# Last MLP layer of a hybrid decoder: down projections of seven blocks as seven quadrant products with tokens on partitions

## The chip, the cores and the metric

One core of a Trainium2 chip (trn2). The metric is the device time of one execution in microseconds, the median of the runs. All arithmetic is in float32: each operand of a large product is split into a high part (type fp32r) and the remainder, and a product is the sum of three matmuls (high x high, high x low, low x high).

## What is computed

Two layers on a residual stream `x` of 512 tokens x 1024 features: multi-head latent attention with its MLP, then gated linear attention with its MLP, then a final RMS norm. The change concerns the second MLP, the end of the mixer before it, and the final norm.

```python
def rms_norm(x, gain):
    y = x * rsqrt(mean(x * x, axis=-1) + EPS)
    return y * gain

def sq_relu_mlp(xn, w_up, w_down):          # w_up (1024, 4096), w_down (4096, 1024)
    hid = square(relu(xn @ w_up))
    return hid @ w_down

for i in range(2):
    x = x + mixer[i](rms_norm(x, norm_mix[i]))     # i = 1: ... @ gla_w_o
    x = x + sq_relu_mlp(rms_norm(x, norm_mlp[i]), mlp_w_up[i], mlp_w_down[i])
return rms_norm(x, final_norm)
```

## The kernel before

The residual stream lies in SBUF with features on partitions: eight tiles `xT[0..7]` of 128 features x 512 tokens, all in one tensor `xall`. The kernel is written in a tile framework: the text states operations and buffers, and a scheduler orders the instructions of each engine ahead of time by their place in the text and by a model of when their inputs are there. Each engine then works through its list in order. `bufs=n` on a tag means n buffers in turn; a new tile waits until the oldest one has been read for the last time.

Weights come with `load` (SyncE's queue, 1 MB, two buffers `wraw`). `piece` splits a part of them into `wh` and `wl` (three buffers each): ScalarE writes the high part (line 104), VectorE the low part (line 107). `mm3` is the three matmuls (lines 112 to 114).

An MLP goes through its 4096 hidden features in eight blocks of 512 (`FB`). For the first block, `up` is a plain product: four tiles of 128 hidden features, 8 x 3 matmuls of 512 tokens each. For the others, `up_fast` multiplies by quadrants: the block's weights (1024 features x 512 hidden) and the normed stream (1024 x 512 tokens) are both cut in four, and seven products of sums and differences of quadrants take the place of eight (Strassen's scheme in Winograd's form). The combinations of the stream, T1 to T4, are made once (`quadrants`), those of the weights by VectorE for each block (s1, s2, s4 and one in place). In one product, each high weight tile is multiplied by the high and low stream parts side by side (512 columns, line 923), each low weight tile by the high part alone (256 columns, line 924). The two halves of the result are added by ScalarE and VectorE on the way out of PSUM (`total`, lines 938 to 941); `finish` applies relu, the norm's factor and the square, and splits the hidden quadrant into its parts.

`down` of a block is a plain product: eight output tiles, each 4 x 3 matmuls of 512 tokens, and each is added to `xT` by VectorE (line 837). It is a generator: `up_fast` of block b+1 calls for its tiles at set places (`others`), so that TensorE always has one of the two to do. In the last block of the last MLP (`down_final`) the first 256 tokens stay with features on partitions and go through the final norm there; the other 256 are turned by transposes into PSUM and get the down products added with tokens on partitions (line 871). Class `Final` does both norms and stores two outputs that the host joins.

At the end of linear attention, `out_start` begins the output projection with two tiles for the first four feature tiles of its input, while the last two heads are still being normed and turned (`head_norm`, `gather`). `out_proj` does the rest of the eight tiles and adds them to `xT`.

Of the kernel before, what the change touches and what calls it, by code (L numbers as in the profile page):

```python
# [50 lines left out]
def trunk_kernel(ctx: ExitStack, tc: tile.TileContext, t_in: dict, out: bass.AP, out_row: bass.AP):  # L51
# [12 lines left out]
    BANKS = {False: {"a": 2, "b": 3, "c": 3}, True: {"b": 3, "c": 1}}  # L64
# [157 lines left out]
    class Norm:  # L222
# [38 lines left out]
        def finish(self):  # L261
            m = bank("c")
# [100 lines left out]
    def a_pair(psums, w, nrm):  # L363
        for k in range(ND):
            if k == 5:
                nrm.finish()
            for j in range(2):
                mm3(psums[j], cut(w[j], slice(None), k), nrm.out[k], k == 0, k == ND - 1)
# [394 lines left out]
    def out_start(w2d, X, n):  # L763
        raw = col_chunk(w2d, 0, 256)
        w = [piece(raw[:, :, j * P : (j + 1) * P], ND, P) for j in range(2)]
        ps_ = [bank("a"), bank("a")]

        def mms(ks):
            for k in ks:
                for j in range(2):  # L770
                    mm3(ps_[j], cut(w[j], slice(None), k), X[k], k == 0, k == ND - 1)

        mms(range(n))
        return ps_, lambda: mms(range(n, ND))

    def out_proj(w2d, X, nxt, begun=None):
        for c in range(4):
            if c == 0:
                ps_, rest = begun or out_start(w2d, X, 0)
                rest()  # L780
            else:
                raw = col_chunk(w2d, c * 256, 256)
                w = [piece(raw[:, :, j * P : (j + 1) * P], ND, P) for j in range(2)]
                ps_ = [bank("ac"[c % 2]), bank("ac"[c % 2])]
                for j in range(2):
                    a_type(ps_[j], w[j], X)
            for j in range(2):
                m = 2 * c + j
                DVE.tensor_tensor(xT[m], ps_[j], xT[m], ALU.add)
                nxt.add(m, xT[m])  # L790


    def mlp(layer, nrm, tag, nxt, final=False):
# [47 lines left out]

        def down_final(b, hid):
            W = []
            for c in range(2):
                raw = load(
                    w_dn[b * FB : (b + 1) * FB, c * 512 : (c + 1) * 512].rearrange("(k p) n -> p k n", p=P), 4, 512
                )
                for k in range(4):  # L850
                    w = both_parts()
                    split(raw[:, k], w[:, 0], w[:, 1])
                    W.append((w[:, 0], w[:, 1]))
            for m in range(ND):
                p = bank("b")[:, :TH]
                for k in range(4):
                    w = cut(W[m // 4 * 4 + k], slice(None), slice(m % 4 * P, (m % 4 + 1) * P))
                    mm3(p, w, cut(hid[k], slice(None), slice(0, TH)), k == 0, k == 3)
                DVE.tensor_tensor(xT[m][:, :TH], p, xT[m][:, :TH], ALU.add)
                nxt.add(m)  # L860
            for t in (2, 3):
                tk = slice(t * P, (t + 1) * P)
                ps_ = [bank("ac"[t % 2]) for _ in range(2)]
                for c in range(2):

                    for j in range(4):
                        PE.matmul(ps_[c][:, j * P : (j + 1) * P], xT[c * 4 + j][:, tk], ident, start=j == 0, stop=False, is_transpose=True, skip_group_check=True)
                    for k in range(4):
                        w, x = cut(hid[k], slice(None), tk), W[c * 4 + k]
                        for n, (a, b_) in enumerate(((w[0], x[0]), (w[0], x[1]), (w[1], x[0]))):  # L870
                            PE.matmul(ps_[c], a, b_, start=False, stop=k == 3 and n == 2, skip_group_check=True)  # L871
                    if (t, c) == (2, 0):
                        nxt.mean()
                    nxt.row(t, c, ps_[c])
                    if (t, c) == (2, 0):
                        nxt.finish()


# [110 lines left out]
        for b in range(NB):  # L989
# [10 lines left out]
            if final:  # L1000
                psum_layout(False)
                down_final(b, hid)
            else:
                for _ in down(b, hid):
                    pass


    def gla(layer, nrm, vtag, ytag):
# [377 lines left out]
        def heads():  # L1386
            for h in (0, 2):
# [33 lines left out]
                if h:  # L1421
                    begun.append(out_start(w_o, Y, 4))
# [82 lines left out]
    class Final:  # L1505
        def __init__(self):
            self.es = ExitStack()
            self.out = None

        def add(self, m):  # L1510
            if self.out is None:
                pool = self.pool = self.es.enter_context(tc.tile_pool(name="fin", bufs=1, reuse_waits="tile"))
                self.out = [pool.tile([P, 2, TH], F32, tag=f"o{c}", name=f"o{c}") for c in range(ND // 2)]
                self.gain = pool.tile([P, D], F32, name="fin_gain")
                SP.dma_start(self.gain, t_in["fin_row"].to_broadcast([P, D]))
                DVE.tensor_scalar(self.gain, self.gain, -0.5, None, ALU.mult)
            src = xT[m][:, :TH]
            if m == 0:
                self.acc = sb.tile([P, TH], F32, tag="acc", bufs=2, name=uname("acc"))
                ACT.activation(self.acc, src, AF.Square)  # L1520
            else:
                sq = tmp((P, TH))
                ACT.activation(sq, src, AF.Square)
                DVE.tensor_tensor(self.acc, self.acc, sq, ALU.add)
                if m == ND - 1:
                    self.sums = parts_of(self.acc, lambda: tmp((P, TH), F32R))
            ACT.activation(self.out[m // 2][:, m % 2], src, AF.Copy, scale=gcol("fin", m))

        def mean(self):
            self.ms = bank("b")[:, :TH]  # L1530
            for i in range(2):
                PE.matmul(self.ms, inv_dr, self.sums[i], start=i == 0, stop=i == 1)

        def finish(self):
            r = sb.tile([P, TH], F32, tag="rstd", bufs=2, name=uname("rstd"))
            rsqrt(r, self.ms, TH)
            o_out = out.rearrange("(j p) t -> p j t", p=P)
            for c in range(ND // 2):
                y = self.out[c]
                for j in range(2):  # L1540
                    DVE.tensor_tensor(y[:, j], y[:, j], r, ALU.mult)
# [85 lines left out]
```

## Time and profile before

| | |
|---|---|
| median of three runs | 1083.77 us (1083.42 to 1083.77) |
| profiled execution | 1084.2 us, its span 1082.2 us |
| granted TensorE clock, mean | 0.998 |
| TensorE busy | 1072.8 us (99%) |
| VectorE busy | 864.5 us (80%) |
| ScalarE busy | 556.2 us (51%) |
| GpSimd busy | 43.7 us (4%), all in the first fifth |
| read from HBM | 98.35 MB, 93 GB/s over the span |

The span runs from the first to the last instruction; the profiled execution's own time is 2.0 us longer. PE is TensorE's matmuls, PEld its weight loads, DVE VectorE, ACT ScalarE, POOL GpSimd, SP SyncE. A row of instructions has the line of the kernel, the engine, the operation, output<-inputs with their shapes, the count, and then busy microseconds and mean nanoseconds of one. Matmuls overlap, so that their single durations add up to more than the time that passes.

### The profile page before, as it was taken

How to read it: one execution, taken by the hardware profiler on the slowest of the kernel's cores; microseconds unless marked ns; L12 is line 12 of the kernel's file. 1: busy time of each engine (PE TensorE's matmuls, PEld its weight loads, DVE VectorE, ACT ScalarE, POOL GpSimd, SP SyncE). 2: the span in 40 equal slices, each digit the busy share in tenths (PEclk: the TensorE clock that was granted, in tenths of full speed). 3: DMA queues.
4: the chain of work that ended last, by engine and by line, in shares of the span. 5: the costliest groups of instructions: out<-in, count | busy, mean ns of one | idle time of the engine just before them, and what ended most of it. 6: DMA issues, size and time to landing. Idle time of an engine off the chain costs nothing.

```text
span 1082.2 us, 14050 instructions
## 1 busy us (share of the span) xinstructions
PE 1072.8 (99%) x5352; PEld 906.4 (84%) x5352; DVE 864.5 (80%) x1446; ACT 556.2 (51%) x947; POOL 43.7 (4%) x72
## 2 busy tenths in 40 slices
PE   9999999999999999999999999999999999999997
PEld 8888888888888888888888888888888888888886
DVE  7899968987887877977686497569888797797885
ACT  7767654553453454445345565655445345344354
POOL 8310002000000000000000000000000000000000
PEclk9999999999999999999999999999999999999999
DMA  7311232142332332322222222142233233223222
GB/s 225 88 50 39 79 115 81 49 146 78 117 117 78 116 118 78 91 86 97 88 78 78 78 78 78 41 154 76 80 117 117 78 109 121 82 80 127 67 98 78
DMA packets 86195, 101.61 MB, mean 94 GB/s; under 512 B 7440, under 2 KB 64016, under 8 KB 86128
## 3 DMA queue, kind: packets, MB, share of 16 engines
q1 hardware_dynamic: 84320, 99.67, 28.3%
q10 hardware_dynamic: 1808, 1.05, 0.3%
q8 instruction: 42, 0.69, 0.3%
q14 instruction: 25, 0.20, 0.1%
HBM read 98.35 MB, written 2.10 MB: 93 GB/s over the span
## 4 chain that ended last, share of the span: by engine, by line
PE 96%; DVE 2%; ACT 1%; DMA 0%; issue 0%; SPq 0%; DVEq 0%; ACTq 0%
PE ps L114 20%; PE ps L112 20%; PE ps L113 20%; PE ps L923 17%; PE ps L924 9%; PE ps L1199 2%; PE ps L129 1%; PE ps L408 1%; PE ps L871 1%; PE ps L1326 1%; PE ps L1249 0%; PE ps L671 0%; PE ps L667 0%; PE ps L670 0%; PE ps L669 0%; DMA gains<-in_gains_dram 0%
## 5 line engine op out<-in xcount | busy, mean ns | idle before, releaser
L112 PE MATMUL ps<-set,wh 128*128 128x512 f32 x760 | 296.6, 390 | 1.1 <-DVE g L1349 0.8
L113 PE MATMUL ps<-set,wh 128*128 128x512 f32 x760 | 296.5, 390 | 0.0
L114 PE MATMUL ps<-set,wl 128*128 128x512 f32 x760 | 296.1, 390 | 0.0
L104 ACT ACTIVATE wh<-wraw 128x1024 fp32r<-128x1024 f32 x139 | 147.0, 1061 | 226.8 <-PE ps L113 114.4
L107 DVE TENSOR_TENSOR wl<-wraw,wh 128x1024 fp32r<-128x1024 f32 x139 | 169.5, 1220 | 34.7 <-ACT wh L104 34.6
L112 PEld LDWEIGHTS ps<-set,wh 128*128 128x128 f32 x760 | 142.6, 188 | 31.2 <-DVE g L1349 1.1
L114 PEld LDWEIGHTS ps<-set,wl 128*128 128x128 f32 x760 | 142.7, 188 | 30.2
L113 PEld LDWEIGHTS ps<-set,wh 128*128 128x128 f32 x760 | 142.8, 188 | 27.6
L923 PE MATMUL ps<-T,wh 128*128 128x512 f32 x448 | 157.5, 391 | 0.0
L924 PE MATMUL ps<-T,wl 128*128 128x256 f32 x448 | 126.2, 282 | 0.0
L923 PE MATMUL ps<-set,wh 128*128 128x512 f32 x336 | 119.9, 397 | 0.0
L923 PEld LDWEIGHTS ps<-T,wh 128*128 128x128 f32 x448 | 84.1, 188 | 18.2
L924 PE MATMUL ps<-set,wl 128*128 128x256 f32 x336 | 94.2, 280 | 0.0
L107 DVE TENSOR_TENSOR wl<-comb,wh 128x1024 fp32r<-128x1024 f32 x42 | 51.3, 1222 | 47.2 <-ACT wh L104 47.2
L837 DVE TENSOR_TENSOR xT<-ps,xT 128x512 f32<-128x512 f32 x120 | 82.2, 685 | 6.7 <-PE ps L114 6.7
L104 ACT ACTIVATE wh<-comb 128x1024 fp32r<-128x1024 f32 x42 | 44.6, 1061 | 83.3 <-PE ps L923 81.8
L924 PEld LDWEIGHTS ps<-T,wl 128*128 128x128 f32 x448 | 84.6, 189 | 0.5
L923 PEld LDWEIGHTS ps<-set,wh 128*128 128x128 f32 x336 | 63.1, 188 | 15.1
L941 DVE TENSOR_TENSOR tmp<-ps,tmp 128x512 f32<-128x512 f32 x98 | 67.1, 685 | 0.9
L924 PEld LDWEIGHTS ps<-set,wl 128*128 128x128 f32 x336 | 63.4, 189 | 1.6
L104 ACT ACTIVATE wh<-raw 128x1024 fp32r<-128x1024 f32 x28 | 29.5, 1054 | 56.7 <-PE ps L923 55.8
L112 PE MATMUL ps<-wh,set 128*128 128x512 f32 x144 | 58.5, 407 | 0.0
(372 smaller groups left out, 1658.3 us busy)
## 6 DMA issues: line engine op xcount, KB each, us to landing
wraw<-in_mlp_w_up_dram SPq DMA_DIRECT2D x32, 1024.0 KB, 5.4
wraw<-in_mlp_w_down_dram SPq DMA_DIRECT2D x18, 1024.0 KB, 5.1
raw<-in_mlp_w_down_dram SPq DMA_DIRECT2D x14, 1024.0 KB, 5.0
wraw<-in_gla_w_in_dram SPq DMA_DIRECT2D x12, 1024.0 KB, 5.2
wraw<-in_mla_w_o_dram SPq DMA_DIRECT2D x4, 1024.0 KB, 5.2
wraw<-in_gla_w_o_dram SPq DMA_DIRECT2D x4, 1024.0 KB, 5.2
xT<-in_x_dram SPq DMA_DIRECT2D x6, 256.0 KB, 5.5
wraw<-in_mla_w_in_dram SPq DMA_DIRECT2D x3, 512.0 KB, 6.4
```

The lines of the kernel that those rows point to most:

```text
L104: order(ACT.activation(hi, src, AF.Copy))
L107: lo_eng.tensor_tensor(lo, src, f(hi), ALU.subtract)
L112: PE.matmul(psum, wh, xh, start=start, stop=False)
L113: PE.matmul(psum, wh, xl, start=False, stop=False)
L114: PE.matmul(psum, wl, xh, start=False, stop=stop)
L129: PE.transpose(psum, src, ident[: src.shape[0], : src.shape[0]])
L408: PE.matmul(p, w[:, i, j * P : (j + 1) * P], x, start=start, stop=stop)
L837: DVE.tensor_tensor(xT[m], p, xT[m], ALU.add)
L923: PE.matmul(o.rearrange("p (h t) -> p h t", h=2), wh, x, start=start and k == 0, stop=False, skip_group_check=True)
L924: PE.matmul(o[:, :TH], wl, x[:, 0], start=False, stop=k == KH - 1, skip_group_check=True)
L941: DVE.tensor_tensor(by_tile(r), high, by_tile(r), ALU.add)
L1199: PE.matmul(p[:, t - t0], k[:, t * P : (t + 1) * P], moving[:, t], start=True, stop=True)
```

## The change

The last MLP gets a function of its own, `mlp_last`; the first one keeps `mlp`.

- The hidden block is no longer split for a plain product. It stays as four quadrants (hidden half x token half, `Q`, two sets in turn), and the down projection of the first seven blocks is also done as seven products of quadrants, with the tokens as the stationary operand and 512 output features as the moving one. Its output therefore has tokens on partitions.
- The partial results of the seven blocks stay in SBUF in five running sums of 128 x 1024 (`S11`, `S12`, `SU`, `S21`, `S5`); four of them lie in the place of `xall`. The stream itself is first written to memory (`x_kept`) and read back in the seventh block.
- `step` does one block: the down products of block b and the up products of block b+1, fourteen in all, which alternate; the diff shows the first seven. The sums of Winograd's scheme that several outputs share are carried on inside PSUM: ScalarE copies a bank into another one (`y`, `w2`, `e`, `d`), and the next products go on adding there. `onto` does the same with a running sum from SBUF.
- In an up product, the high weight tile meets the high and the low part of the stream in two matmuls of 256 columns, and all three terms add up in one place of PSUM.
- Part of the weights' combinations is made while loading: a plain load by SyncE and then a load by GpSimd that adds (`accum_op`) into the same tile. Each tile is loaded again for the next block as soon as it has been read for the last time (`after`).
- The last block's down product is done with tokens on partitions for all tokens; the old stream is turned into PSUM, added to the sums and carried on from there. The final norm follows by rows, and there is one output.
- The out projection of linear attention begins with three tiles, in banks "b", "c" and "a"; the second load of weights is therefore kept for its second tile.

```diff
-    BANKS = {False: {"a": 2, "b": 3, "c": 3}, True: {"b": 3, "c": 1}}
+    BANKS = {False: {"a": 2, "b": 3, "c": 3}, True: {"b": 3, "c": 1}, "quad": {"u": 4}}
...
-    def out_start(w2d, X, n):
-        raw = col_chunk(w2d, 0, 256)
-        w = [piece(raw[:, :, j * P : (j + 1) * P], ND, P) for j in range(2)]
-        ps_ = [bank("a"), bank("a")]
+    def out_start(w2d, X, n, tags="aa"):
+        raws, w, ps_ = [], [], []
+        for m, tag in enumerate(tags):
+            if m % 2 == 0:
+                raws.append(col_chunk(w2d, m * P, 256))
+            w.append(piece(raws[-1][:, :, m % 2 * P : (m % 2 + 1) * P], ND, P))
+            ps_.append(bank(tag))
...
-                    begun.append(out_start(w_o, Y, 4))
+                    begun.append(out_start(w_o, Y, 4, "bca"))
...
+    def mlp_last(layer, nrm):
...
+        x_kept = dram.tile([P, ND, S], F32, name="x_kept")
+        SP.dma_start(x_kept, xall)
+
+        Q = [[[f(slot("B")) for _ in range(2)] for _ in range(2)] for _ in range(2)]
...
+        def comb():
+            return fast.tile([P, 2 * S], F32, tag="comb", bufs=6, name=uname("comb"))
...
+        def signed(src, hi, lo, sign):
+            ACT.activation(hi, src, AF.Copy, scale=sign)
+            DVE.scalar_tensor_tensor(lo, src, sign, f(hi), ALU.mult, ALU.subtract)
...
+        def finish(src, half, th, q):
+            r = tmp()
+            r_t = nrm.rstd[:, (first, second)[th]].unsqueeze(1).to_broadcast([P, 2, TH])
+            DVE.scalar_tensor_tensor(by_tile(r), by_tile(src), 0.0, r_t, ALU.min if half else ALU.max, ALU.mult)
+            ACT.activation(q[half][th], r, AF.Square)
...
+        def fetch(b, name):
+            if name in ("A1", "A2"):
+                c = int(name[1]) - 1
+                W[name] = col_chunk(w_up, (b + 1) * FB + c * 256, 256)
+                if c:
+                    POOL.dma_start(W[name][:, :KH], up_quadrant(b, 0, 0), accum_op=ALU.add)
+                return
+            q = up_quadrant if name == "S1" else down_quadrant
+            W[name] = t = by_k(comb(), KH if name == "S1" else 2)
+            plain, more = {
+                "d11": ((0, 0), None), "d12": ((0, 1), None), "d22": ((1, 1), None),
+                "S1": ((1, 1), (1, 0)), "dS1": ((1, 1), (1, 0)), "dS3": ((1, 0), (0, 0)),
+            }[name]
+            SP.dma_start(t, q(b, *plain))
+            if more:
+                POOL.dma_start(t, q(b, *more), accum_op=ALU.add)
+
+        def up_product(t, a, q, start):
+            w = piece(a, KH, 256)
+            for j in range(2):
+                o = t[:, j * TH : (j + 1) * TH]
+                for k in range(KH):
+                    wh, wl = cut(w, slice(None), k, slice(j * P, (j + 1) * P))
+                    xh, xl = quad[q][k][:, 0], quad[q][k][:, 1]
+                    for n, (a_, x_) in enumerate(((wh, xh), (wh, xl), (wl, xh))):
+                        PE.matmul(o, a_, x_, start=start and j == 0 and k == 0 and n == 0, stop=k == KH - 1 and n == 2, skip_group_check=True)
+
+        def down_product(t, a, parts, start):
+            wh, wl = piece(a, 2, 512)
+            for tt in range(2):
+                o = t[:, tt * 512 : (tt + 1) * 512]
+                for k in range(2):
+                    xh, xl = cut(parts, slice(None), slice(k * TH + tt * P, k * TH + (tt + 1) * P))
+                    for n, (x_, w_) in enumerate(((xh, wh[:, k]), (xh, wl[:, k]), (xl, wh[:, k]))):
+                        PE.matmul(o, x_, w_, start=start and k == 0 and n == 0, stop=k == 1 and n == 2, skip_group_check=True)
+
+        def step(b, q, r, after):
+            opening = b == 0
...
+            def begun(src, total):
+                if opening:
+                    ACT.activation(total, src, AF.Copy)
+                    return two_banks("e")
+                t = two_banks("e")
+                ACT.activation(t, src, AF.Copy)
+                return t
+            def add(total, t):
+                DVE.tensor_tensor(total, t, total, ALU.add)
+            def onto(tag, total, a, parts):
+                t = two_banks(tag)
+                if not opening:
+                    ACT.activation(t, total, AF.Copy)
+                down_product(t, a, parts, opening)
+                ACT.activation(total, t, AF.Copy)
...
+            z = bank("u")
+            up_product(z, a11, "11", True)
+            y = bank("u")
+            ACT.activation(y, z, AF.Copy)
+            d = two_banks("d")
+            down_product(d, d11, parts_of_quad(q11), True)
+            e = begun(d, S11)
+            up_product(y, a12, "21", False)
+            finish(y, 0, 0, r)
+            DVE.tensor_tensor(a11, s1, a11, ALU.add)
+            down_product(e, d12, parts_of_quad(q21), opening)
+            add(S11, e)
+            DVE.tensor_tensor(d11, ds1, d11, ALU.add)
+            DVE.tensor_tensor(q12, q22, q12, ALU.subtract)
+            DVE.tensor_tensor(q11, q11, q12, ALU.add)
+            up_product(z, a11, "T2", False)
+            u = tmp()
+            ACT.activation(u, z, AF.Copy)
+            DVE.tensor_tensor(a12, a11, a12, ALU.add)
+            down_product(d, d11, parts_of_quad(q11, -1.0), False)
+            e = begun(d, S12)
+            DVE.tensor_tensor(d12, d11, d12, ALU.add)
+            after("d11")
+            w = bank("u")
+            up_product(w, s1, "T1", True)
...
+        for b in range(NB - 1):
+            step(b, Q[b % 2], Q[(b + 1) % 2], ...)
...
+        def residual(t, c):
+            src = (S11, S12, S21, SU)[2 * c + t // 2][:, t % 2 * 512 : (t % 2 + 1) * 512]
+            p = bank("u")
+            for j in range(4):
+                m = 4 * c + j
+                tr(p[:, j * P : (j + 1) * P], kept[m // 2][:, m % 2, t * P : (t + 1) * P])
+            DVE.tensor_tensor(src, p, src, ALU.subtract if c else ALU.add)
...
+            ACT.activation(o, src, AF.Copy)
...
+        order = [(t, c) for c in range(2) for t in range(NT)]
+        residual(*order[0])
+        residual(*order[1])
+        for i, tc_ in enumerate(order):
+            if i + 2 < len(order):
+                residual(*order[i + 2])
+            row(*tc_)
...
-    fin = Final()
-    psum_layout(True)
-    mlp(1, n_mlp1, "B", fin, True)
-    fin.es.close()
+    psum_layout("quad")
+    mlp_last(1, n_mlp1)
```

More of the change, by code (lines that the diff above doesn't have):

```diff
@@ L793, in mlp, with add @@
-    def mlp(layer, nrm, tag, nxt, final=False):
+        ps_, raws, rest = begun or out_start(w2d, X, 0)
+        rest()
+        def add(m, p):
+            DVE.tensor_tensor(xT[m], p, xT[m], ALU.add)
+            nxt.add(m, xT[m])
+        for m, p in enumerate(ps_):
+            add(m, p)
+        for c in range(len(ps_) // 2, ND // 2):
+            raw = raws[c] if c < len(raws) else col_chunk(w2d, c * 256, 256)
+            tiles = range(max(2 * c, len(ps_)), 2 * c + 2)
+            done = [(piece(raw[:, :, m % 2 * P : (m % 2 + 1) * P], ND, P), bank("ac"[c % 2])) for m in tiles]
+            for w, p in done:
+                a_type(p, w, X)
+            for m, (w, p) in zip(tiles, done):
+                add(m, p)
```

314 lines of the change are left out of this document (189 added, 125 removed).

## The prediction

> **What bounds the kernel now.** I read the page's head and its chain of waits first, then the busy time by stretches of the last MLP layer, then the order of time on TensorE there.
>
> ```profile
> span 1082.2 us, 14050 instructions
> PE 1072.8 (99%) x5352; PEld 906.4 (84%) x5352; DVE 864.5 (80%) x1446; ACT 556.2 (51%) x947; POOL 43.7 (4%) x72
> PE 96%; DVE 2%; ACT 1%; DMA 0%; issue 0%; SPq 0%; DVEq 0%; ACTq 0%
> ...
> 890.00:931.00 41.00, 41.00 (x208) 34.87 (x207) 33.43 (x45) 18.19 (x27) 0.00 (x0) 1.00 0.30 103
> 1050.88:1075.83 24.95, 24.93 (x164) 22.42 (x162) 14.61 (x37) 10.71 (x28) 0.00 (x0) 1.00 0.17 62
> 1075.83:1082.20 6.37, 0.00 (x0) 0.00 (x0) 1.76 (x5) 1.70 (x5) 0.00 (x0) 0.70 0.23 89
> ```
>
> The stretch rows give length, then busy time of PE, PEld, DVE, ACT and POOL, then granted clock, DMA share and GB/s. In the MLP blocks TensorE has no idle time at full clock (41.00 of 41.00), and the chain that ended last is 96% matmuls. So a matmul removed is time saved, as long as VectorE (33.4 of 41) and ScalarE (18.2) still deliver in time.
>
> A busy matmul overlaps the next one, so I price matmuls by the distance between starts.
>
> ```profile
> 683.58 0.39 PE L112 MATMUL ps<-wh,set 128*128 128x512 f32 x1
> 688.80 0.40 PE L114 MATMUL ps<-wh,set 128*128 128x512 f32 x1
> ...
> 761.21 0.39 PE L923 MATMUL ps<-set,wh 128*128 128x512 f32 x1
> ...
> 1040.21 0.39 PE L112 MATMUL ps<-set,wh 128*128 128x512 f32 x1
> 1050.42 0.39 PE L112 MATMUL ps<-set,wh 128*128 128x512 f32 x1
> 1051.10 0.28 PE L112 MATMUL ps<-set,set 128*128 128x256 f32 x1
> 1059.73 0.28 PE L112 MATMUL ps<-set,set 128*128 128x256 f32 x1
> 1062.49 0.28 PE L114 MATMUL ps<-set,set 128*128 128x256 f32 x1
> 1066.39 3.01 PE L871 MATMUL ps<-set,set 128*128 128x512 f32 x12
> 1069.60 3.03 PE L871 MATMUL ps<-set,set 128*128 128x512 f32 x12
> ```
>
> - 512 columns, weights stationary: 1040.21 to 1050.42 is 45 steps, 0.227 us each.
> - 512 columns, tokens stationary (the form the new down products use): 683.58 to 688.80 is 23 steps, 0.227; in the last stage twelve take 3.01 with a last one of 0.39, so (3.01-0.39)/11 = 0.238. I take 0.231, nearer the first, which has the same operands.
> - 256 columns: 1059.73 to 1062.49 is 23 steps, 0.120.
> - The seven blocks that are changed run from 761.21 (first fast up product) to 1051.10 (last block's down): 289.9 us, 41.41 a block.
>
> **The change: TensorE in the seven blocks.** Before, one block is 56 matmuls of 512 with 56 of 256 (up) and 96 of 512 (down, 96 x 0.227 = 21.8). The up part is thus 41.41-21.8 = 19.6. After, up is 7 products x 2 tiles x 4 x 3 = 168 matmuls of 256: 168 x 0.120 = 20.2, 0.6 more, since the wide product that did two terms at once is cut in two. Down is 7 products x 2 x 2 x 3 = 84 of 512: 84 x 0.231 = 19.4 (19.1 at 0.227, 20.0 at 0.238). Sum 39.6 a block (39.3 to 40.2), 1.8 less; times seven 12.7 us saved, between 8.5 and 14.8. The Trainium skill (TensorE: Matmul & The Clock Gate, Back-to-back issue gap) gives N/2.4 + 2.5 ns for an isolated matmul, 0.216 and 0.109 us; by that the block would go from 38.9 to 36.5 and 17 us would be saved. The rows stand about 0.011 above both, so the trace decides for the smaller sum.
>
> **What has to keep up.** Each product is now 24 x 0.120 = 2.9 or 12 x 0.231 = 2.8 us, fourteen to a block, and each needs its own piece of weights split by ScalarE, then VectorE.
>
> ```profile
> L107 DVE TENSOR_TENSOR wl<-wraw,wh 128x1024 fp32r<-128x1024 f32 x139 | 169.5, 1220 | 34.7 <-ACT wh L104 34.6
> L104 ACT ACTIVATE wh<-wraw 128x1024 fp32r<-128x1024 f32 x139 | 147.0, 1061 | 226.8 <-PE ps L113 114.4 <-PE ps L923 62.9 <-PE ps L114 19.0
> L938 ACT ACTIVATE tmp<-ps 128x512 f32<-128x512 f32 x56 | 32.5, 580 | 0.0
> ...
> 705.65 2.01 ACT L104 ACTIVATE wh<-wraw 128x1024 fp32r<-128x1024 f32 x2 [3.42 <-PE ps L113]
> 884.84 1.22 DVE L970 TENSOR_TENSOR wraw<-wraw,wraw 128x1024 f32<-128x1024 f32 x1
> 885.98 0.68 DVE L837 TENSOR_TENSOR xT<-ps,xT 128x512 f32<-128x512 f32 x1
> 1044.82 2.18 ACT L104 ACTIVATE set<-wraw 128x512 fp32r<-128x512 f32 x4
> 1046.56 2.48 DVE L107 TENSOR_TENSOR set<-wraw,set 128x512 fp32r<-128x512 f32 x4
> ```
>
> Back to back, VectorE takes 1.14 for 1024 elements (884.84 to 885.98) and (2.48-0.68)/3 = 0.60 for 512; ScalarE 2.01-1.06 = 0.95 and (2.18-0.62)/3 = 0.52.
>
> VectorE in a block after: of 1024, 14 pieces, 4 weight combinations and 3 additions onto running sums (21 x 1.14 = 23.9); of 512, 7 splits of hidden quadrants, 4 hidden combinations, 4 finishes and 2 sums (17 x 0.60 = 10.2). Together 34.1 of 39.6, against 33.4 of 41 now: the eight evictions and ten sums of the old form nearly pay for the new work. ScalarE: 14 pieces and 6 copies of 1024 (20 x 0.95 = 19.0), 15 of 512 (7.8): 26.8 of 39.6, against 18.2 now. No engine but TensorE is full.
>
> Waits that are added: a sum is carried from one PSUM bank into another by ScalarE (0.58 for 512, about 1.0 for 1024) and TensorE goes on adding there. In the order of the text another product of 2.8 us always lies between the product that is copied and the one that needs the copy, so a copy costs nothing unless over 1.7 us of other work is queued ahead of it on ScalarE, where it waits behind at most a split or two (0.95 each). Without that cover each would cost about a microsecond. With three buffers for pieces, a piece can be split once the third product before it is done: two products (5.6 us) of lead for 1.06 + 1.22.
>
> The tight place is the start of a block. Until its sixth product, at 14.2 us, VectorE has 4 pieces, 3 weight combinations and one sum of 1024 (8 x 1.14) and 7 operations of 512 (4.2): 13.3 of 14.2. There I expect a late piece: 0 to 1 us a block, 0.4 taken, 3 us in all. Behind a VectorE instruction that waits for a transfer or for TensorE stand the next pieces, and TensorE for those.
>
> **Loads.** POOL, idle here until now, gets four accumulating loads of 512 KB a block, each behind a plain load of SP into the same tile; in all 7 MB a block instead of 4.
>
> ```profile
> wraw<-in_mlp_w_up_dram SPq DMA_DIRECT2D x32, 1024.0 KB, 5.4
> wraw_v<-in_mla_w_ukv_dram SPq DMA_DIRECT2D x2, 512.0 KB, 5.1
> ```
>
> No row shows an accumulating load. Tightest is the pair for the down weights' sum: its tile is free some 25 us into a block and wanted about 50 us in, so plain (5.1) and accumulating load may take 25 together; and four one after another fit in a block up to 9.9 each. Nearest is 5.1, so I put them at nothing; at the far end they become the second slow rival. The Trainium skill (DMA: Bandwidth & Descriptors, Anatomy of one DMA) has 2.0 us + bytes/436 GB/s for a transfer issued by GpSimd: 3.2 us here, as an estimate and without the adding. The share 0.30 of the stretch row becomes 0.30 x 7/4 x 41/39.6 = 0.54 at the same price per byte. The spill of the residual (2 MB, two times 5.4) lies beside the first up projection (96 x 0.227 = 21.8), its return beside the seventh block; without cover each would cost 11 us once.
>
> **The end.** Last block: 24.95 now. After, eight row halves, each 4 transposes and 12 matmuls as now 1066.39 to 1069.60 = 3.21: 25.7, 0.7 more. The first needs transposes, a VectorE addition (0.68) and a ScalarE copy (0.58) before its matmuls, with only the next transposes beside them: 1.0 more (0 to 2). The tail of 6.4 us keeps its steps (square, gain, reciprocal root, scale, store): 0, within 0.3.
>
> **The out projection begun with three tiles.** Linear attention's end leaves small holes.
>
> ```profile
> 692.52 0.51 PE L112 MATMUL ps<-set,wh 128*128 128x512 f32 x1 [0.85 <-DVE g L1349]
> ...
> 700.05 0.73 PE L112 MATMUL ps<-set,wh 128*128 128x512 f32 x2 [0.25 <-ACT set L1368]
> ```
>
> The first hole is the wait for bank "a", still being read by the gating; the new order begins on "b". Twelve more matmuls of fill (2.7) can close both, 1.1 saved. Against that the three tiles hold all three piece buffers: the fourth tile's piece can only begin when the first tile's last product is done, 6 x 0.227 = 1.4 before the group ends, and its low half needs 1.06 + 1.22 = 2.3: about 0.9 lost (the 3.42 of ScalarE's idle time above is the same wait, which today has the third buffer as cover). I take 0, between -1.1 and +0.9.
>
> **Sum.** -12.7 + 3 + 0.7 + 1.0 + 0 = -8.0. The profiled run took 1084.2 us (span 1082.2 and 2.0 around it), 0.4 above the median 1083.77 of the three runs. 1084.2 - 8.0 = 1076.2, as a median 1075.8; I say 1075.5.
>
> **Rivals.**
> - Everything covered: no late pieces (-3), 14.8 instead of 12.7, holes closed (-1.1): about 1069 to 1071. For it: today's blocks lose nothing at all with VectorE at 82%. Against: VectorE at 86%, uneven in the block. Chance 0.15.
> - VectorE becomes the bound, slower than before. Today's block leaves it 41.0-33.4 = 7.6 us idle, part of it forced waits for matmuls or ScalarE. If the longer chains (hidden split after combination, sum after product) force the same 7.6, a block is 34.1 + 7.6 = 41.7, 0.3 longer than now: 1083.8 + 7 x 0.3 + 1.7 = 1088. It turns the sign from 41.41 - 0.24 - 34.1 = 7.1 us of forced idle a block. Against: the waits today are those of an engine that is ahead. Chance 0.15.
> - The accumulating loads are the bound. At 11 us each, four in a row take 44 us, 4.4 over the block: with six blocks so loaded 1075.5 + 26 = 1102. It begins above 9.9 each, twice the nearest row. Chance 0.05.
> - Stalls eat the gain: 0.9 to 1.5 us a block more than the 0.4 taken, 1082 to 1086. Chance 0.07.
> - That the change does less than it says can hardly be: the matmul counts are fixed by the loops.
>
> **How the numbers follow.** The forecast (1071 to 1081) has 0.58. Faster by over 0.2% (2.2 us, about what a measurement of this kernel can tell from no change) is the forecast and the covered case: 0.73. Within 0.2%: 0.07. Slower: 0.20. The forecast's own range is 1071 to 1081; for 8 in 10 the range goes down to 1068.5 (the covered case) and up to 1087, into the second rival.
>
> **What would show it.** Right: TensorE still 99% busy; seven blocks at 39.3 to 40.4 us from the first quadrant product to the next block's; matmuls of 256 at 0.120 and of 512 at about 0.231; VectorE 34 and ScalarE 27 us a block; last block near 27; no wait of TensorE for a piece (VectorE's low half) longer than 1 us. Wrong: TensorE waits for pieces in every block (VectorE bound), VectorE's weight sums waiting for POOL's loads (transfers bound), down products at 0.24 or more, or holes between products for ScalarE's copies.

## The result: 1.2% slower, and the profile after

| | before | after |
|---|---|---|
| median | 1083.77 us (1083.42 to 1083.88, four runs) | 1096.45 us (1094.33 to 1098.03, four runs) |
| ratio to before | | 1.0116 [1.0103, 1.0128] |
| profiled execution, its span | 1084.2, 1082.2 us | 1098.03, 1096.3 us |
| seven changed blocks | 761.21 to 1051.10: 289.9 us | 762.51 to 1054.25: 291.7 us |
| last block, to its last matmul | 24.7 us | 1054.25 to 1089.60: 35.4 us |
| tail | 6.4 us | 6.7 us |

The forecast of 1075.5 has the wrong sign, and 1096.45 lies above the range. The profiled execution of after is the slowest of its four, 1.6 above their median; 1.7 of its surplus arises in the first 11 us, far ahead of the changed code: 0.3 because the first matmul of line 408 starts later (5.91 against 5.59), the rest because these matmuls start 0.43 us apart until 9.91, and in before only until 6.60; after that it is 0.23 in both. Why this slow stretch lasted longer in this execution the traces don't show. At the out projection 0.4 are won back. Otherwise the 14.1 us lie in two places: +1.8 in the seven blocks (where -9.7 was forecast) and +10.6 in the last block (where +1.7 was forecast).

The page's head and chain of waits, after:

```profile
span 1096.3 us, 14765 instructions
PE 1067.1 (97%) x5626; PEld 912.9 (83%) x5626; DVE 871.5 (79%) x1394; ACT 625.7 (57%) x1009; POOL 75.9 (7%) x100
PE 78%; DMA 11%; DVE 6%; ACT 2%; issue 2%; POOL 0%; DVEq 0%; SPq 0%; POOLq 0%; ACTq 0%
```

TensorE was 99% busy and is 97%; 11% of the chain that ended last is now transfers, which had 0%. The stretches (length; busy PE, PEld, DVE, ACT, POOL; granted clock, DMA share, GB/s), first of before, then of after:

```profile
761.21:1051.10 289.89, 289.89 (x1457) 246.30 (x1456) 240.90 (x323) 133.84 (x199) 0.00 (x0) 1.00 0.30 100
```

```profile
762.51:1054.25 291.74, 277.91 (x1769) 251.43 (x1768) 247.02 (x274) 199.62 (x254) 31.01 (x25) 0.99 0.68 172
805.63:848.97 43.34, 40.81 (x253) 37.06 (x252) 34.99 (x39) 28.30 (x36) 6.04 (x5) 0.96 0.71 172
888.79:928.71 39.92, 39.29 (x254) 35.66 (x252) 34.89 (x39) 28.29 (x36) 4.95 (x4) 1.00 0.74 185
1054.25:1060.50 6.25, 3.36 (x22) 2.72 (x20) 6.25 (x9) 2.85 (x5) 0.00 (x0) 0.79 0.00 0
1060.50:1073.07 12.57, 11.48 (x46) 8.98 (x44) 4.55 (x11) 4.16 (x10) 0.00 (x0) 0.83 0.00 1
```

TensorE's own work did shrink by 12.0 us (289.9 to 277.9), but it now stands idle for 13.8 (291.74-277.91). VectorE (34.9 of 39.9) and ScalarE (28.3) are where the forecast put them. What TensorE waited for, all over the run (in total, times, longest):

```profile
PE ps L1092 <- DVE wl L107: 9.7, 7, 2.5
PE ps L129 <- DVE xT L1253: 2.9, 2, 2.3
PE ps L1101 <- DVE wl L107: 2.0, 1, 2.0
PE ps L1267 <- DVE xT L1271: 1.9, 1, 1.9
PE ps L1092 <- ACT ps L1133: 1.5, 1, 1.5
PE ps L1267 <- ACT ps L1257: 1.4, 2, 1.1
```

The first row is the greater part of the loss in the blocks: seven waits of an up product for a low half, 1.4 us each on the average. Six of them stand in the third product of the second to the seventh block, one (2.04) in the fifth product of the first. The third and the fifth row and 0.7 for a high half stand in the first and the seventh block; with the first row they make up the 13.8. VectorE's waits name what is behind the first row:

```profile
DVE comb L1145 <- DMA comb<-in_mlp_w_down_dram: 21.1, 7, 5.7
```

Line 1145 is `d11 += ds1`; seven times VectorE waits there for a load, 3.0 us each. One instance, in the block that starts at 888.79, on VectorE, on TensorE, then on GpSimd, then two pieces of the chain of waits, and last the times to landing of the plain loads of `dS3` and `dS1` (the shorter one is that of `dS1`):

```profile
890.41 0.68 DVE L107 TENSOR_TENSOR set<-set,set 128x512 fp32r<-128x512 f32 x1
893.01 1.23 DVE L1145 TENSOR_TENSOR comb<-comb,comb 128x1024 f32<-128x1024 f32 x1 [1.92 <-DMA comb<-in_mlp_w_down_dram]
894.16 1.22 DVE L107 TENSOR_TENSOR wl<-wraw,wh 128x1024 fp32r<-128x1024 f32 x1
```

```profile
895.43 0.39 PE L1092 MATMUL ps<-set,wl 128*128 128x256 f32 x1 [0.63 <-DVE wl L107]
```

```profile
877.73 0.37 SPq L1080 DMA_DIRECT2D comb<-in_mlp_w_down_dram  x1
```

```profile
881.97 2.53 POOL L1082 DMA_DIRECT2D comb<-in_mlp_w_down_dram  x2 [11.35 <-DMA comb<-in_mlp_w_down_dram]
```

```profile
871.97 9.44 DMA comb<-in_mlp_w_down_dram
...
883.30 9.62 DMA comb<-in_mlp_w_down_dram
```

```profile
DMA to landing us min/median/max: 5.0/7.2/9.4
```

In order of time: the tile of `dS1` comes free and its plain load goes out at 877.73, 28.8 us into the block before; it takes 5.0 and lands at 882.7. Its adding load is the second in GpSimd's list: the one for `dS3` stands ahead, and GpSimd waits 11.35 us for the plain load of that (871.97 to 881.41). This place in the list costs nothing here: the adding load of `dS3` goes out 0.56 us after its plain load has landed, and that of `dS1` at 883.30, as long after its own. It lands at 892.92. VectorE was free for the sum at 891.1 (893.01 less the 1.92 of idle time). Behind the sum in its list is the low half (894.16 to 895.38) that TensorE's third product needs, and TensorE goes on at 895.43. Between the issue of the plain load and the place of the sum in VectorE's list lie 13.4 us; the two loads with the 0.6 between them took 15.2.

The page's issue list, from issue to landing:

```profile
comb<-in_mlp_w_down_dram SPq DMA_DIRECT2D x35, 512.0 KB, 5.2
...
comb<-in_mlp_w_down_dram POOLq DMA_DIRECT2D x14, 512.0 KB, 9.6
```

The end, on TensorE and on VectorE:

```profile
1054.25 1.47 PE L129 MATMUL ps<-ident,comb 128*128 128x128 f32 x12
1058.00 1.12 PE L129 MATMUL ps<-ident,comb 128*128 128x128 f32 x4 [2.28 <-DVE xT L1253]
1059.73 1.12 PE L129 MATMUL ps<-ident,comb 128*128 128x128 f32 x4 [0.62 <-DVE xT L1253]
1060.50 10.61 PE L1267 MATMUL ps<-set,set 128*128 128x512 f32 x36
1070.95 1.03 PE L129 MATMUL ps<-ident,comb 128*128 128x128 f32 x8
```

```profile
1053.78 1.22 DVE L1235 TENSOR_TENSOR xT<-xT,sum 128x1024 f32<-128x1024 f32 x1
1054.92 1.29 DVE L107 TENSOR_TENSOR set<-set,set 128x512 fp32r<-128x512 f32 x2
1056.12 1.22 DVE L1240 TENSOR_TENSOR xT<-xT 128x1024 f32<-128x1024 f32 x1
1057.26 0.68 DVE L1253 TENSOR_TENSOR xT<-ps,xT 128x512 f32<-128x512 f32 x1
1057.86 1.22 DVE L1241 TENSOR_TENSOR xT<-xT,sum 128x1024 f32<-128x1024 f32 x1
1058.99 3.07 DVE L1253 TENSOR_TENSOR xT<-ps,xT 128x512 f32<-128x512 f32 x5
```

Twenty transposes run before the first row's matmul at 1060.50, since the transposes of the next rows stand ahead of it in TensorE's list and wait for banks that VectorE has to empty. VectorE is busy for all of the 6.25 us: the closing sums (lines 1235, 1240, 1241) and the last hidden splits come before its residual additions (line 1253). TensorE, left with little to do, has a granted clock of 0.79 there and of 0.83 in the next stretch, so that 36 matmuls take 10.45 us (1060.50 to 1070.95), 0.290 each on the average. Shorter stretches show what these means are made of, the clock at half and then at full; the last row is the one other slow stretch in the changed code, behind TensorE's wait of 2.53 us in the second block:

```profile
1059.00:1064.00 5.00, 4.38 (x13) 3.57 (x13) 3.06 (x6) 1.74 (x3) 0.00 (x0) 0.50 0.00 0
1067.00:1070.00 3.00, 3.00 (x14) 2.51 (x14) 0.00 (x0) 0.00 (x0) 0.00 (x0) 1.00 0.00 0
815.60:818.90 3.30, 3.30 (x16) 3.11 (x15) 3.30 (x4) 0.94 (x1) 0.00 (x0) 0.50 0.00 0
```

### The profile page after: what moved, and what is told of

Read it like the earlier page. It is cut to its first block, busy times and chain, and to the rows that moved or that the text cites. A ratio compares the mean times of both kernels' runs of the same rounds, so it can differ in the third digit from the quotient of the medians.

```text
span 1096.3 us, 14765 instructions
## 1 busy us (share of the span) xinstructions
PE 1067.1 (97%) x5626; PEld 912.9 (83%) x5626; DVE 871.5 (79%) x1394; ACT 625.7 (57%) x1009; POOL 75.9 (7%) x100
## 4 chain that ended last, share of the span: by engine, by line
PE 78%; DMA 11%; DVE 6%; ACT 2%; issue 2%; POOL 0%; DVEq 0%; SPq 0%; POOLq 0%; ACTq 0%
PE ps L112 15%; PE ps L114 15%; PE ps L113 15%; DMA comb<-in_mlp_w_down_dram 9%; PE ps L891 8%; PE ps L1092 6%; PE ps L1101 5%; PE ps L892 4%; DVE wl L107 2%; PE ps L1267 2%; PE ps L129 2%; PE ps L1492 1%; PE ps L408 1%; DMA wraw<-in_mlp_w_down_dram 1%; PE ps L1619 1%
## 5 line engine op out<-in xcount | busy, mean ns | idle before, releaser
L112 PE MATMUL ps<-set,wh 128*128 128x512 f32 x536 | 209.1, 391 | 0.5 <-ACT set L1661 0.3
L113 PE MATMUL ps<-set,wh 128*128 128x512 f32 x536 | 209.2, 391 | 0.0
L114 PE MATMUL ps<-set,wl 128*128 128x512 f32 x536 | 208.8, 390 | 0.0
L1101 PE MATMUL ps<-wh,set 128*128 128x512 f32 x392 | 129.7, 392 | 0.7 <-ACT wh L104 0.7
L112 PEld LDWEIGHTS ps<-set,wh 128*128 128x128 f32 x536 | 100.6, 188 | 22.3 <-ACT wh L104 1.0
L114 PEld LDWEIGHTS ps<-set,wl 128*128 128x128 f32 x536 | 100.6, 188 | 21.5 <-DVE wl L107 0.4
L113 PEld LDWEIGHTS ps<-set,wh 128*128 128x128 f32 x536 | 100.7, 188 | 19.6
L1101 PEld LDWEIGHTS ps<-wh,set 128*128 128x128 f32 x392 | 74.0, 189 | 15.3 <-ACT wh L104 0.9
L1092 PE MATMUL ps<-T,wh 128*128 128x256 f32 x448 | 79.9, 279 | 0.0
L1101 PE MATMUL ps<-wl,set 128*128 128x512 f32 x196 | 77.2, 394 | 2.0 <-DVE wl L107 2.0
L891 PE MATMUL ps<-T,wh 128*128 128x512 f32 x224 | 78.7, 391 | 0.0
L1092 PE MATMUL ps<-set,wh 128*128 128x256 f32 x336 | 62.5, 286 | 1.5 <-ACT ps L1133 1.5
L891 PE MATMUL ps<-set,wh 128*128 128x512 f32 x168 | 60.0, 397 | 0.0
L112 PE MATMUL ps<-wh,set 128*128 128x512 f32 x144 | 58.5, 406 | 0.0
L1092 PEld LDWEIGHTS ps<-set,wh 128*128 128x128 f32 x336 | 54.3, 194 | 3.5 <-ACT ps L1133 1.9
```

The costliest lines, as they stand in the source:

```text
L112: PE.matmul(psum, wh, xh, start=start, stop=False)
L113: PE.matmul(psum, wh, xl, start=False, stop=False)
L114: PE.matmul(psum, wl, xh, start=False, stop=stop)
L891: PE.matmul(o.rearrange("p (h t) -> p h t", h=2), wh, x, start=start and k == 0, stop=False, skip_group_check=True)
L1092: PE.matmul(o, a_, x_, start=start and j == 0 and k == 0 and n == 0, stop=k == KH - 1 and n == 2, skip_group_check=True)
L1101: PE.matmul(o, x_, w_, start=start and k == 0 and n == 0, stop=k == 1 and n == 2, skip_group_check=True)
```

## The experiments

The theory from the two traces: prices of matmuls, VectorE and ScalarE hold, and the time went (a) in each block, into one sum of weights that waits for an adding load at the head of VectorE's list, and (b) at the end, into the closing sums ahead of the first row, with a slower clock behind the pause. The rivals: VectorE is simply too full for the new blocks (the forecast's second rival), so that moving an instruction within its list changes nothing; or transfers at a share of 0.7 are the bound by themselves. In the kernels with a line added near the top of the file, lines stand two further down.

**The sum behind the low half.** Same work on every engine; only the place of line 1145 in VectorE's list changes.

```
-        lo_eng.tensor_tensor(lo, src, f(hi), ALU.subtract)
+        low[0] = lo_eng.tensor_tensor(lo, src, f(hi), ALU.subtract).ins
...
-            DVE.tensor_tensor(d11, ds1, d11, ALU.add)
+            with tc.issue_after(low[0]):
+                DVE.tensor_tensor(d11, ds1, d11, ALU.add)
```

> The sum of two down-weight quadrants (d11 += dS1) is issued on VectorE behind the low half of the fourth product's piece, and not ahead of the third product's; nothing else changes. Theory A (the second, adding load of dS1 lands some 4 us into the block, and the sum that waits for it stands ahead of the third product's low half in VectorE's list): TensorE's waits for a low half at the third product, 9.7 us in seven blocks, go to under 2; blocks near 39.4 us instead of 39.8 to 41.1; 1088 to 1090 us. Rival R1 (VectorE is full in the first half of a block, whatever the loads do): the waits move to the fifth or sixth product and the time stays within 2 us of 1096.

Measured: 1081.14 us (1079.61 to 1082.74, ten runs), ratio to before 0.9974 [0.9965, 0.9984]; 15.3 less than the change as it was made. The seven blocks, 39.05 us from the middle of them (the length of one block), and TensorE's one remaining wait for a low half:

```profile
761.20:1036.55 275.35, 274.42 (x1771) 249.89 (x1769) 246.71 (x274) 200.31 (x254) 31.01 (x25) 1.00 0.72 182
871.51:910.56 39.05, 39.05 (x254) 35.61 (x253) 34.89 (x38) 28.39 (x35) 4.76 (x4) 1.00 0.75 189
```

```profile
PE ps L1094 <- DVE wl L109: 0.9, 1, 0.9
```

Idle time of TensorE falls from 13.8 to 0.9 with VectorE as busy as it was (246.7 against 247.0) and the DMA share no lower (0.72 against 0.68). So neither VectorE's load nor the transfers' bound the blocks; the order of one instruction did. The gain is larger than expected for two reasons. The waits at the first block's start and in the last one went too, and TensorE's busy time fell by 3.5 us at the same matmuls. Of these, 1.5 lie in the block in which the granted clock was 0.96 (40.81 busy, against 39.29 in the other block shown); the rest goes with the waits themselves, since a block with one wait is busy for 39.29 at clock 1.00 and a block without one for 39.05.

**No second term.** This asks whether the adding loads cost anything beyond that one wait: all four of a block are left out, and with them the second term of the weights' sums. The sum on VectorE stands in its old place.

```
-                if c:
-                    POOL.dma_start(W[name][:, :KH], up_quadrant(b, 0, 0), accum_op=ALU.add)
...
-            if more:
-                POOL.dma_start(t, q(b, *more), accum_op=ALU.add)
```

> The four adding loads of GpSimd in each block are left out (the weights' sums then lack their second term); everything else, the sums on VectorE too, stays. Theory A: no wait at the third product, blocks at 39.2 to 39.4 us, 1087 to 1089 us. R1: the same waits as now, 1094 to 1097. If the volume of the transfers as such held back something else (the first block, the last one), another 2 to 3 us less: 1085.

Measured: 1079.86 us (1079.22 to 1080.0, five runs), ratio 0.9962 [0.9947, 0.9976]. That is 5 us below the lowest time expected, as the late sum was 7 below its own. It is 1.3 below the kernel with the late sum: once the sum stands in the right place, the adding loads cost hardly anything more.

**The same loads without the adding.** Same issue, queue and bytes; a transfer from GpSimd overwrites, so that the first term of the sums is lost.

```
-                    POOL.dma_start(W[name][:, :KH], up_quadrant(b, 0, 0), accum_op=ALU.add)
+                    POOL.dma_start(W[name][:, :KH], up_quadrant(b, 0, 0))
...
-                POOL.dma_start(t, q(b, *more), accum_op=ALU.add)
+                POOL.dma_start(t, q(b, *more))
```

> The same four loads of GpSimd as plain loads that overwrite instead of adding (the weights' sums then lack their first term). If the adding is what takes 9.6 us to land, they land in about 5 us like SyncE's 512 KB loads and the waits at the third product are under 0.5 us each, as without the loads. If GpSimd's queue or its place among the other transfers takes the time, they land in 9 to 10 us and the waits of 0.5 to 2.5 us stay.

One execution: 1080.58 us. Of VectorE's seven waits at line 1145 one is left, 3.0 us in the first block, and of TensorE's waits for a low half one of 1.1. The queues (packets, MB, share of 16 engines) and issues from 800 to 1000 us, first of this kernel, then of the one with the late sum, which still adds:

```profile
q0 software_dynamic: 3128, 11.37, 18.1%
...
comb<-in_mlp_w_down_dram POOLq DMA_DIRECT2D x10, 512.0 KB, 6.3
wraw<-in_mlp_w_up_dram POOLq DMA_DIRECT2D x6, 512.0 KB, 4.1
...
comb<-in_mlp_w_up_dram POOLq DMA_DIRECT2D x5, 512.0 KB, 4.2
```

```profile
q0 software_dynamic: 8462, 11.37, 34.0%
...
comb<-in_mlp_w_down_dram POOLq DMA_DIRECT2D x10, 512.0 KB, 9.3
wraw<-in_mlp_w_up_dram POOLq DMA_DIRECT2D x5, 512.0 KB, 9.2
...
comb<-in_mlp_w_up_dram POOLq DMA_DIRECT2D x5, 512.0 KB, 6.2
```

At the same 11.37 MB the adding loads come as 2.7 times as many packets, hold the DMA engines nearly twice as long, and land 2.0 to 5.1 us later. The plain ones land near the 5 us that were expected if the adding is what takes the time. By these medians, as an estimate, the pair above would have taken 15.2-(9.6-6.3) = 11.9 without the adding, and fitted into its 13.4 us.

**The end in another order.** The first two residuals are added before the last product of the seventh block, and the closing sums of lines 1240 and 1241 come behind the first row. The last hidden splits also change their order, with the sum of line 1235 between them. The blocks are left as they are.

```
             finish(z, 1, 0, r)
+            if b == NB - 2:
+                residual(0, 0)
+                residual(1, 0)
...
-        residual(*order[0])
-        residual(*order[1])
         for i, tc_ in enumerate(order):
             if i + 2 < len(order):
                 residual(*order[i + 2])
             row(*tc_)
+            if i == 0:
+                DVE.tensor_tensor(S21, S21, SU, ALU.add)
+                DVE.tensor_tensor(SU, SU, S5, ALU.add)
```

> The first two row halves of the last block get their residual (transposes, addition, copy into PSUM) in the text ahead of the seventh block's last product, and the closing sums S21 += SU and SU += S5 come after the first row instead of ahead of it. Theory B (TensorE stands still 4.9 us at the start of the last block because the additions queue on VectorE behind the closing sums, and the clock granted then falls to about 0.8): the stretch from the end of the seventh block to the last matmul goes from 35.4 us to 27 to 29, clock 1.00, 1088 to 1090 us. Rival (the rows themselves are slow, since each waits for its bank to be read): the stretch stays above 32 and the time above 1093.

Measured: 1090.81 us (1089.71 to 1092.55, four runs), ratio 1.0064 [1.0049, 1.0079]; 5.6 less than after, and 0.8 above the range expected. From 1053.95 to the last matmul's end at 1083.16 are 29.2 us, 6.1 less than after. The stretch at the end's start, and what TensorE still waited for:

```profile
1053.95:1060.00 6.05, 5.96 (x37) 5.01 (x36) 6.05 (x10) 2.85 (x6) 0.00 (x0) 1.00 0.00 0
```

```profile
PE ps L1092 <- DVE wl L107: 10.6, 7, 2.1
PE ps L1268 <- DVE xT L1272: 3.5, 2, 2.0
```

VectorE is still busy all through those 6 us, but TensorE is too, and its clock stays at 1.00. The second row, 3.5 us, is banks that come free too late behind the row's own last steps. The first shows the blocks' waits nearly as they were (10.6 against 9.7). The edit moves the first residuals and the closing sums together; what each is worth alone was not tried.

**Both.** The late sum and the new order of the end in one kernel, by the two edits above.

> The late sum and the reordered end together. If the two losses are separate (theories A and B, in different stages), the gains add: 1081.1 less 5.6, 1075 to 1077 us. If one only uncovers the other, 1079 or more.

Measured: 1075.95 us (1075.2 to 1077.6, five runs), ratio 0.9926 [0.9913, 0.9940]. Together they take off 20.5, the two alone 15.3 and 5.6: two separate losses. That the time is next to the 1075.5 of the forecast is luck: seven blocks take 275.6 (761.63 to 1037.26), which saves 14.3 where 9.7 was forecast, and the end takes 30.7 (to 1067.98), which costs 6.0 where 1.7 was forecast.

**A version with a cheaper end.** The late sum stays. Instead of adding the residual to the running sum and copying that into PSUM, the residual is transposed into the row's own bank and the matmuls are added there; the running sum comes in on the way out.

```
+            o = bank("u")
+            for j in range(4):
+                m = 4 * c + j
+                PE.matmul(o[:, j * P : (j + 1) * P], kept[m // 2][:, m % 2, t * P : (t + 1) * P], ident, start=j == 0, stop=False, is_transpose=True, skip_group_check=True)
...
+            DVE.tensor_tensor(y, o, y, ALU.subtract if c else ALU.add)
+            ACT.activation(sq, y, AF.Square, accum_out=stat[:, c : c + 1])
```

> The late sum, and an end without the copy into PSUM: each row half's residual is transposed into its own bank and the matmuls add to it there; the running sum from SBUF is added by VectorE afterwards, before the square. No product of the last block then waits for VectorE or ScalarE. Theory B: the stretch from the end of the seventh block to the last matmul is 8 x 3.2 = 25.7 to 26.5 us instead of 34.7, the clock stays at 1.00, and the tail grows by one addition of 0.7: 1072 to 1074 us. Rival (the rows are limited by ScalarE's and VectorE's reading of the banks): stretch above 29, no better than the reordered end.

Measured: 1071.89 us (1071.27 to 1072.14, four runs), ratio 0.9887 [0.9873, 0.9900]: faster than both kernels, and just below the range expected. The end up to its last matmul:

```profile
1037.59:1063.20 25.61, 25.36 (x125) 20.59 (x123) 16.85 (x36) 10.07 (x25) 0.00 (x0) 1.00 0.11 42
```

With the start chain gone the end takes the 25.6 us that its rows cost by the forecast's prices (25.7).

**Three tiles alone.** The kernel before, with nothing but the out projection begun with three tiles.

```
-                    begun.append(out_start(w_o, Y, 4))
+                    begun.append(out_start(w_o, Y, 4, "bca"))
```

> The kernel before with only the out projection of linear attention begun with three tiles, in banks b, c and a. By the holes of that stage (0.85 and 0.25 us, and a late fourth tile): between 1.1 us faster and 0.9 us slower; by the trace of the changed kernel (74.8 us from the last states to the norm against 75.2) 0.4 us faster: 1083.0 to 1083.9.

Measured: 1083.64 us (1083.07 to 1084.28, eleven runs) against 1084.11 for before in the same series, ratio 0.9996 [0.9987, 1.0005]: no difference that can be told. The hole of 0.85 for the gating is gone; what it won is below what the runs can tell.

**Two tiles in the version with the cheaper end.**

> The same as the version with the late sum and the end without copies, but with the out projection begun with two tiles as in the kernel before. If three tiles are worth 0.4 us, this one is 0.4 us slower than that version; if the fourth tile's late piece eats it, the same within 0.3 us.

Measured: 1071.74 us (1071.02 to 1073.11, four runs), ratio 0.9888 [0.9874, 0.9901], the same as with three tiles. The hole for the gating (line 1631 there) is back, 0.8 us, and costs what the runs can't tell.

## Why the prediction was wrong

**TensorE's work in the blocks: the mechanism right, the saving just past its range.** With the wait out of the way seven blocks hold 274.4 us of TensorE, 39.2 each and 39.05 where no wait falls; 39.6 (39.3 to 40.2) was forecast. So the term of -12.7 (-8.5 to -14.8) would have been -15.5 (289.9 to 274.4).

**VectorE and ScalarE per block: right.** 34.9 and 28.3 against 34.1 and 26.8; neither is near the 39.05 of a block. The second rival, VectorE as the bound with 41.7 us a block, is refuted by the late sum: 39.3 us a block (275.35/7) with the same VectorE work.

**Loads, put at nothing: the step that failed.** It said of the sum's tile that it "is free some 25 us into a block and wanted about 50 us in", and put the adding load near the plain load's 5.1. All three numbers were off in the same direction. The tile came free at 28.8 us. It was wanted at 42.1 (891.1-848.97, the start of the block in which it was fetched): I had read "wanted" from the sum's place in the text, behind the fourth product, while in VectorE's list it stood ahead of the third product's low half. That left 13.4 us where I saw 25. And the adding load took 9.6, where the nearest row, a plain load of 5.1, had been put in its place; the plain load ahead of it took the 5.0 that was forecast. It needed both errors: two loads of 5.1 with the 0.6 between them are 10.8 and would have fitted into 13.4, and the 15.2 that they took would have fitted into 25. The late sum mends the one, the loads without the adding mend the other, and either takes away nearly all of the waits. The DMA share, 0.54 by the forecast at the same price per byte, was 0.74 in the block shown. The Trainium skill (DMA: Bandwidth & Descriptors, Anatomy of one DMA) would give an estimate of 3.2 us for such a load without the adding; these traces have 4.1 to 6.3 without the adding and 6.2 to 9.6 with it. The Trainium skill (Collectives: The Full Stack, Stop ④ — SDMA + CCE: where bytes move and the add happens) describes the add of a DMA engine, for the step of a collective, as read, read, write "with the add free in between". What is free there is the addition and not the second read, so that the nearly doubled share of the software queue above does not speak against it; that the second read is what these loads into SBUF pay for, no run here shows.

The rival of adding loads had the right place and the wrong threshold. It asked when four loads in a row would fill a block (9.9 each); they took 9.6, below it, and the loss came all the same, since one load missed its own time, by 1.9 us in the instance above. The sign to look for stood in the last lines of the forecast ("VectorE's weight sums waiting for POOL's loads"), with a chance of 0.05.

**The late piece at a block's start: right place, wrong cause and size.** 0.4 us a block was taken for an uneven VectorE; 13.8 us in all came, and nearly all of it went with the one sum. With that moved, the blocks lose 0.9 in all, so the uneven VectorE that the forecast feared costs next to nothing.

**The end, +0.7 for the rows: right** (25.6 in the version with the cheaper end, against 25.7). **The start chain, +1.0 (0 to 2): the second step that failed.** The last block took 35.35, 9.65 over the rows' 25.7. By the rows above: 2.9 of waits of TensorE for the residual additions; 1.6 because its 20 transposes took 3.36 instead of 20 x 0.088 (four take 0.35 in the version with the cheaper end, at full clock); 2.1 because 36 matmuls took 10.45 instead of 36 x 0.231; and 3.3 of later waits for banks (1.9 and 1.4): 9.9 in all. I had counted the first row's own chain (0.68 and 0.58) and not what VectorE had ahead of it: three closing sums of 1024 and two hidden splits, 4.6 of the 5.2 us from 1053.78 to the second residual addition at 1058.99. That the clock would fall behind the pause was no part of the sum at all. Nor is the queue of closing sums the whole cause: 20 transposes, where 4 are needed, stand ahead of the first row, and the version that leaves VectorE and ScalarE out of the row's start has no such loss, with the closing sums in their old place in the text.

The granted clocks of 0.79 and 0.83 are means of stretches that are partly at half: from 1059.00 to 1064.00 it was 0.50, from 1067.00 to 1070.00 it was 1.00. The Trainium skill (TensorE: Matmul & The Clock Gate, Part 1) has two states, full and half, with half after an idle window of about 3.4 us. The two states agree with these rows. No pause here is that long: half followed on one of 2.28 us between transposes and on one of 2.53 us between matmuls, while behind waits of 2.04 and 1.96 us in the first and the seventh block the clock stayed at 1.00. The measurement decides: a pause shorter than 3.4 us can cost a slow stretch behind it. From which length on, these runs don't settle.

**Three tiles, at 0 (-1.1 to +0.9): right**; the interval of the ratio, 0.9987 to 1.0005, holds 1. **The tail, at 0 within 0.3: right** (6.7 against 6.4).

Sum of the misses in the profiled execution: 11.5 in the blocks, 8.9 in the last block, 0.3 in the tail, and 1.3 ahead of the blocks (1.7 in the first 11 us less 0.4 at the out projection); 22.0, against 14.1 measured and -8.0 forecast. That the gain was there to be had, the version with the late sum and the cheaper end shows: 1071.89, near the case in which everything is covered (1069 to 1071), though with another end than the one that was forecast. Still open: the longer slow stretch in the first 11 us, and how much of the 9.6 is the adding and how much the other traffic beside it (the plain load of `dS3` took 9.4 in the instance above, 5.2 in the median). An earlier plain load by way of a seventh `comb` buffer was not tried.

## What to carry to other kernels

When an engine works through a list in order, ask of every instruction that waits for a transfer where it stands in that list, not in the text, and what stands behind it; a sum that nobody needs yet can stop the feed of the engine that bounds the kernel. Moving it behind the next thing that is needed cost nothing here and was worth 15 us. Count a chain of loads from the moment its buffer comes free to the place of its reader in the list, and do not put the price of a plain transfer on one that adds. For the start of a stage count all that the helping engine still has to finish, not only the new chain.

## What the runs showed of the hardware

- A 512 KB load that adds into SBUF took 6.2 to 9.6 us (medians) from issue to landing beside other traffic, the same loads without adding 4.1 to 6.3. The packets were smaller (11.37 MB in 8462 against 3128), and the DMA engines' share was 34.0% against 18.1%.
- The granted clock was 0.50 from 1059.00 to 1064.00, behind pauses of 2.28 and 0.62 us with only transposes between, and 0.50 from 815.60 to 818.90, behind a pause of 2.53 us between matmuls. The 36 matmuls of 512 columns after the first of these took 0.290 us on the average instead of 0.231. Short waits of TensorE thus cost more than their own length: without them the seven blocks' busy time was 3.5 us less at the same matmuls.
- Four transposes into a bank to which matmuls are then added take 0.35 us in the version with the cheaper end (1040.32 to 1040.67), and no copy into PSUM is needed.
